# Twenty pairs of column blocks of h @ w_in, each by seven half products in place of eight, with gates and partial sums kept in DRAM and the convolution's norm moved behind the attention

## The chip, the cores and the metric

The kernel runs on one core of one Trainium2 chip. The metric is the device time of one launch in microseconds (us). Before the change two timed runs gave 2034.66 and 2035.71 us, so the median is 2035.18 us.

Engines are named as the profile names them: PE is TensorE (PEld its weight loads), DVE is VectorE, ACT is ScalarE, POOL is GpSimd, SP is SyncE, whose queue issues every DMA of this kernel.

## The reference, cut to what matters

Two layers (DEPTH 2) work on 512 tokens of 1024 channels in float32:

```python
h = rms_norm(x, norm_g)
z = h @ w_in                      # 1024 x 14848
(c_glu, c_gate, r_q, r_k, r_v, r_gate, a_q, a_k, a_v, a_gate, g_logit) = split(z)
y_conv = conv_module(c_glu, c_gate, ...) @ w_conv_out     # a*sigmoid(b), 31 taps, layer norm, silu, * silu(c_gate)
y_ret  = retention_branch(r_q, r_k, r_v, r_gate, ...) @ w_ret_out   # 4 heads, both directions, * silu(r_gate)
y_attn = window_attention_branch(...) @ w_attn_out        # 16 heads, 4 kv heads, window 128, * silu(a_gate)
g = sigmoid(g_logit + b_gate)
x = x + (g[0] * y_conv + g[1] * y_ret + g[2] * y_attn) @ w_out
```

## The kernel before, in words

**Products.** Every operand of a product is split into a high and a low part in the fp32r format (`hilo`, and for weights `weights`), and a product is the sum of three matmuls, high by high, high by low, low by high (`mm3`). A block of 128 output columns for all 512 tokens (`columns`, `proj`) takes 8 blocks of 128 input channels, so 24 matmuls with a 128x128 weight tile standing still and 512 tokens streaming through, all summed in one PSUM bank of the pool `pc`. Values, keys and queries are computed with the tokens on the partitions (`tokens`, `tokens256`); the queries' matmuls stream 256 columns, and there are 768 of them in the program.

**Weights.** The weights lie in DRAM in 156 blocks of 128x1024 a layer, in the order of use. One block is loaded by one DMA into `wraw` (3 buffers), its high part `wh` is made by ACT, its low part `wl` by DVE, each in one instruction of 128x1024.

**A layer.** `layer` runs four retention heads (`head`), then the convolution's norm (`conv_stats`, `conv_finish`), the attention (`attention`), and the merge and output projection (`finish`). `self.fill` names what is put between the stages of a head: the convolution's input blocks (`conv_in`: a pair of column blocks b and a, a tanh, a product, and 31 taps on DVE) and the gates of the convolution (`CG`). The retention's gate is four column blocks a head. `ATT_FILL` names what is put between the 16 steps of the attention: gates of the attention (A), merge gates (G), queries (Q) and the convolution's output projection (C). Results that are needed later, such as the taps' sums `y`, the gates and the partial sum `merged`, stay in SBUF.

**Order.** Nothing is issued in the order in which it is written. `Plan.record` notes each instruction with its place in the program (in ns of PE's work) and an offset of urgency; `Plan.order` then walks through a planned time, and lets each engine take the most urgent instruction whose operands are there and whose tiles have room, by the prices of `Plan.cost`. The result is one fixed order for each engine. Each engine then works through its own queue in order and waits on semaphores, so a late instruction holds up all behind it on its engine. Important offsets: loads are 20 us ahead of their place (LOAD_EARLY), weight splits 16 us, reads out of PSUM 20 us (EVAC_EARLY); the taps are 60 us late (TAPS_LATE), so they fill DVE's free time.

**Numbers in names.** `record` calls every instruction from one line, so all have line L318 in the profile (L334 after the change). They are told apart by their tiles: `pc` and `ps` are PSUM banks, `big` holds 128x4x512 arrays, `mid`, `pp` and `th` 128x512 tiles, `wide` the attention's scores, `pads` the padded rows for the taps.

Of the kernel before, what the change touches and what calls it, by code (L numbers as in the profile page):

```python
# [11 lines left out]
F32 = mybir.dt.float32  # L12
# [7 lines left out]
NK = D // P  # L20
EPS = 1e-6
# [13 lines left out]
LOAD_EARLY, SPLIT_EARLY, TAPS_LATE, STATS_LATE = -20000, -16000, 60000, 15000  # L35
# the order of the attention's gates (A), merge gates (G), queries (Q) and the convolution's projection (C) between its steps
ATT_FILL = ["C0", "C1 Q1", "C2", "C3", "C4", "C5 Q2", "C6", "C7", "A0 G0", "Q3 A1", "A2 G1", "A3 G2", "G3", "A4 G4", "A5 G5", "G6", "G7", "A6 A7"]

# columns of the combined input projection
# [4 lines left out]
# columns of the packed parameters  # L44
# [3 lines left out]
# columns of the packed constants  # L48
# [5 lines left out]
class View:  # L54
    """A part of a tile that is allocated when its first instruction is issued.

    ix holds the numbers of the elements that it covers, with the partitions in two halves."""
# [27 lines left out]
    def reshape(self, *shape):  # L85
        """Free dimensions split or joined in order."""
# [58 lines left out]
class Plan:  # L145
    """Records the instructions, orders them, and issues them to Tile in that order.

    Every engine takes, whenever it is free, the most urgent of the instructions whose operands are
    there and whose tiles have room; the engines take turns at a bank of PSUM. Urgency is the place in the program, in ns of the tensor
    engine's work, and an offset. Tiles with one tag are given room in the order of the program, so  # L150
    an order always exists."""


    def __init__(self, nc):
        self.nc = nc
        self.ops = []
        self.now = 0.0
        self.offset = 0.0
        for name in ("tensor", "vector", "scalar", "gpsimd", "sync"):
            setattr(self, name, Engine(self, name))  # L160
# [7 lines left out]
    def cost(self, engine, method, kw):  # L168
        out = kw.get("out")
        n = out.size if isinstance(out, View) else 0  # L170
        if method == "dma_start":
            return 60
        if engine == "tensor":
            if method == "transpose":
                return 107
            f32 = kw["rhs"].tile.dt == F32
            return max(n, 256 if n > 1 else 64) * (4 if f32 and n > 1 else 1) / 2.4
# [20 lines left out]
    def record(self, engine, method, kw):  # L198
# [8 lines left out]
        for writes, v in sorted(views, key=lambda x: x[0]):  # L207
# [3 lines left out]
            # a start of accumulation clears the whole bank's marks: it comes behind what the bank holds  # L211
# [29 lines left out]
    def order(self):  # L241
# [12 lines left out]
        while len(result) < len(ops):  # L254
# [4 lines left out]
            for e in names:  # L259
# [3 lines left out]
                if free[e] <= t:  # L263
# [15 lines left out]
                    if item is not None:  # L279
# [5 lines left out]
                        free[e] = t + op.cost  # L285
                        op.end = t + op.cost + (LATENCY if e != "sync" else 0)
# [3 lines left out]
                        if op.method == "dma_start":  # L290
                            n = max(v.size for v in op.args.values() if isinstance(v, View))
                            dma_free = max(dma_free, t) + n * P * 4 / 350
                            op.end = dma_free + 2000
# [39 lines left out]
class Pair:  # L333
    """A [128, 8, 512] array in two tiles of four rows each."""  # L334
# [4 lines left out]
    def __getitem__(self, k):  # L339
        return self.t[k // 4][:, k % 4, :]  # L340


class Builder:
    def __init__(self, nc, tc, ctx, io):
# [9 lines left out]
        self.pools["xd"] = Pool(ctx, tc, "xd", NK, space=bass.MemoryType.DRAM)  # L354

# [27 lines left out]
    def ps1(self):  # L383
        return self.tile("ps1", [P, S])

# [1 line left out]
    def weights(self, key):  # L387
# [3 lines left out]
        wh = self.tile("wh", [P, 1024], F32R)  # L391
        wl = self.tile("wl", [P, 1024], F32R)
        with nc.urgency(2 * FIRST + FIRST_STEP * (i - 0.1) if i < 4 else LOAD_EARLY):
            nc.sync.dma_start(out=raw, in_=self.io["wpk"][i])
        with nc.urgency(SPLIT_EARLY):
            nc.scalar.copy(out=wh, in_=raw)
            nc.vector.tensor_tensor(out=wl, in0=raw, in1=wh.bitcast(F32), op=ALU.subtract)
        return wh, wl

# [1 line left out]
    def mm(self, out, a, b, start, stop):  # L401
        self.nc.tensor.matmul(out=out, lhsT=a, rhs=b, start=start, stop=stop)

    def mm3(self, out, a, b, start, stop):
        """out (+)= (ah + al)^T (bh + bl), without al^T bl."""
        (ah, al), (bh, bl) = a, b
        self.mm(out, ah, bh, start, False)
        self.mm(out, ah, bl, False, False)
        self.mm(out, al, bh, False, stop)

    def columns(self, key, src, pool="pc"):
        """128 columns of src @ w, channels on partitions."""
# [10 lines left out]
    def rows(self, p, t, k, w, c):  # L423
        """adds the part of row k to 128 tokens' columns of src @ w_in."""
# [3 lines left out]
    def tokens(self, col):  # L428
        """512 columns of src @ w_in with tokens on partitions."""
# [8 lines left out]
    def tokens256(self, col):  # L438
        """256 columns of src @ w_in with tokens on partitions, two blocks of tokens in a bank."""
# [20 lines left out]
    def silu2(self, out, p):  # L460
        """2 silu(p) = (1 + tanh(p / 2)) p"""
        th = self.th()
        with self.nc.urgency(EVAC_EARLY):
            self.nc.scalar.activation(out=th, in_=p, func=AF.Tanh, scale=0.5)
            self.nc.vector.scalar_tensor_tensor(out=out, in0=th, scalar=1.0, in1=p, op0=ALU.add, op1=ALU.mult)

# [1 line left out]
    def rstd_of(self, acc, diag):  # L468
        """acc: [128, 512] sums of squares, to be added over the partitions."""
        nc = self.nc  # L470
        p = self.ps1()
# [8 lines left out]
        pr = self.ps1()  # L480
        self.mm(pr, self.ones, diag, True, True)
        return r, pr

# [27 lines left out]
    def new_input(self, l):  # L511
        """Room for a layer's input, scaled by the norm's gain and split."""
# [5 lines left out]
    def take(self, k):  # L518
        """x[k]: x[k] * g split, and its squares into the running sum."""
# [12 lines left out]
    def layer(self, l):  # L532
# [3 lines left out]
        self.merged = self.pair()  # L536
        CA = self.conv_in
        self.fill = {(0, 0): [lambda: CA(0)], (0, 1): [lambda: CA(1)], (0, 2): [lambda: CA(2)],
                     (1, 0): [lambda: CA(3)], (1, 1): [lambda: CA(4)], (1, 2): [lambda: CA(5)],
                     (2, 1): [lambda: CA(6)], (2, 2): [lambda: CA(7)],  # L540
                     (3, 1): [lambda: self.CG(0), lambda: self.CG(1)], (3, 2): [lambda: self.CG(2)]}
        for h in range(4):
            self.head(h, h == 0)
        self.conv_finish()
# [3 lines left out]
    def filler(self, *at):  # L548
        for f in self.fill.get(at, []):
            f()  # L550

    def normalise(self):
        """h = RMSNorm(x), split."""
        nc = self.nc
        self.rstd, pr = self.rstd_of(self.acc, self.pp())
# [6 lines left out]
        for k in range(NK):  # L562
            h = self.t2()
# [526 lines left out]
```

## Time and profile before

| what | value |
|---|---|
| timed runs | 2034.66 and 2035.71 us, median 2035.18 |
| span of the profiled execution | 2032.9 us, so 2.3 us of the median lie outside the span |
| PE busy, share of the span | 2021.1 us, 99% (9436 matmuls) |
| DVE busy | 1425.8 us, 70% |
| ACT busy | 834.9 us, 41% |
| DMA | 184.29 MB, mean 91 GB/s, 27.9% of the 16 engines' time for the main queue |
| granted TensorE clock | 1.000 |

The profile is of one execution. The page's first block gives busy times; the chain of work that ended last says which engine sets the end; the groups give, for each kind of instruction, its count, its total busy time and the mean time of one; the waits name who waited for whom; the timeline gives start times. Matmuls are pipelined: the profile gives a 128x512 matmul some 390 ns from start to end, though the next one starts about 230 ns later. The step from one start to the next is what a matmul costs, and it has to be taken from the timeline.

### The profile page before, as it was taken

What the parts mean: (1) busy time and instruction counts of PE and PEld (TensorE: products, weight loads), DVE (VectorE), ACT (ScalarE), POOL (GpSimd) and SP (SyncE); (2) the same over time, 40 slices, a digit from 0 to 9 for tenths busy, and PEclk for the clock granted to TensorE, in tenths of its full rate; (3) what the DMA queues carried; (4) which work ended last, traced back from release to release, by engine and by line L of the source; (5) the groups of instructions that cost most, each with busy time, mean ns of one, the idle gap of its engine ahead of it and who ended that gap; (6) DMA issues with size and microseconds to landing.
All of it is one profiled execution on the core that took longest, in us unless ns stands there. A gap on an engine that the chain in (4) does not pass through costs nothing.

```text
span 2032.9 us, 24260 instructions
## 1 busy us (share of the span) xinstructions
PE 2021.1 (99%) x9436; PEld 1661.8 (82%) x9436; DVE 1425.8 (70%) x2254; ACT 834.9 (41%) x1361; POOL 56.9 (3%) x62
## 2 busy tenths in 40 slices
PE   8999999999999999999999999999999999999999
PEld 6888888888788888888888888888888888888887
DVE  8788887588575556665567888875885755576652
ACT  5323223233344556673332332232333445566731
POOL 0000000000000000000000000000000000000000
PEclk9999999999999999999999999999999999999999
DMA  5322232222232222223432222222222322222232
GB/s 214 101 73 92 82 94 92 70 86 67 89 94 94 81 75 73 63 82 121 166 99 91 83 92 82 94 93 73 83 73 85 97 88 83 65 82 73 92 106 83
DMA packets 53683, 184.29 MB, mean 91 GB/s; under 512 B 6080, under 2 KB 6336, under 8 KB 53568
## 3 DMA queue, kind: packets, MB, share of 16 engines
q1 hardware_dynamic: 53568, 182.75, 27.9%
q8 instruction: 74, 1.21, 0.2%
q14 instruction: 41, 0.34, 0.0%
HBM read 178.53 MB, written 4.19 MB: 90 GB/s over the span
## 4 chain that ended last, share of the span: by engine, by line
PE 99%; DVE 0%; DMA 0%; issue 0%; ACT 0%; SPq 0%; DVEq 0%
PE pc L318 71%; PE ps L318 29%; DMA big<-xT 0%; DVE wl L318 0%; DVE wide L318 0%; SPq L318 0%; DVE pp L318 0%; ACT pp L318 0%; ACT big L318 0%; DVE sm_m L318 0%; DVEq L318 0%
## 5 line engine op out<-in xcount | busy, mean ns | idle before, releaser
L318 PE MATMUL pc<-big,wh 128*128 128x512 f32 x4096 | 1300.5, 397 | 0.0
L318 PEld LDWEIGHTS pc<-big,wh 128*128 128x128 f32 x4096 | 764.6, 188 | 177.8 <-issue 1.9
L318 PE MATMUL pc<-big,wl 128*128 128x512 f32 x2048 | 811.4, 396 | 0.3 <-DVE wl L318 0.3
L318 ACT CAST wh<-wraw 128x1024 fp32r<-128x1024 f32 x312 | 327.2, 1050 | 800.9 <-PE pc L318 531.9
L318 DVE TENSOR_TENSOR wl<-wraw,wh 128x1024 fp32r<-128x1024 f32 x312 | 380.6, 1222 | 212.0 <-ACT wh L318 210.3
L318 PEld LDWEIGHTS pc<-big,wl 128*128 128x128 f32 x2048 | 384.5, 188 | 91.1 <-DVE wl L318 0.8
L318 DVE SCALAR_TENSOR_TENSOR big<-pads,prm,big 128x512 f32<-128x512 f32 x480 | 340.4, 745 | 1.3
L318 PE MATMUL ps<-wh,big 128*128 128x512 f32 (+1 forms) x1152 | 295.4, 345 | 7.4 <-ACT big L318 7.4
L318 PEld LDWEIGHTS ps<-wh,big 128*128 128x128 f32 x1152 | 200.2, 189 | 35.6 <-ACT big L318 7.4
L318 PE MATMUL ps<-wl,big 128*128 128x512 f32 (+1 forms) x576 | 198.6, 346 | 0.0
L318 PEld LDWEIGHTS ps<-wl,big 128*128 128x128 f32 x576 | 108.9, 189 | 14.6 <-issue 0.5
L318 PE MATMUL ps<-big 128*128 128x512 f32 (+2 forms) x448 | 96.2, 344 | 0.2
L318 PEld LDWEIGHTS ps<-big 128*128 128x128 f32 x448 | 80.7, 188 | 15.6 <-DVE sm_m L318 0.9
L318 PE MATMUL ps<-big,pp 128*128 128x512 f32 x384 | 88.5, 389 | 0.0
L318 PEld LDWEIGHTS ps<-big,pp 128*128 128x128 f32 x384 | 72.1, 188 | 15.3
L318 DVE CUSTOM_DVE_ANT_0 wide<-ps,cst,prm 128x256 f32<-128x256 f32 (+1 forms) x128 | 66.1, 548 | 20.6 <-PE ps L318 19.9
L318 ACT CAST pp<-ps 128x512 fp32r<-128x512 f32 x80 | 46.0, 583 | 74.5 <-PE ps L318 73.9
L318 ACT ACTIVATE wide<-wide,sm_m 128x257 f32<-128x257 f32 (+1 forms) x128 | 70.5, 556 | 6.7 <-DVE sm_m L318 6.7
L318 DVE TENSOR_TENSOR big<-ps,big 64x512 fp32r<-64x512 f32 (+2 forms) x80 | 52.8, 662 | 26.0 <-ACT big L318 20.4
L318 DVE TENSOR_TENSOR pp<-ps,pp 128x512 fp32r<-128x512 f32 x80 | 54.3, 687 | 12.9 <-ACT pp L318 12.5
L318 ACT ACTIVATE wide<-wide,sm_d 128x256 f32<-128x256 f32 (+1 forms) x128 | 62.2, 557 | 2.0 <-DVE sm_d L318 2.0
L318 ACT ACTIVATE big<-mid 128x512 fp32r<-128x512 f32 x64 | 40.0, 630 | 39.0 <-DVE mid L318 39.0
(98 smaller groups left out, 1255.5 us busy)
## 6 DMA issues: line engine op xcount, KB each, us to landing
wraw<-wpk SPq DMA_DIRECT2D x312, 512.0 KB, 3.5
wide<-toe SPq DMA_DIRECT2D x16, 448.0 KB, 3.4
big<-xT SPq DMA_DIRECT2D x8, 256.0 KB, 5.1
pp<-xT SPq DMA_DIRECT2D x8, 256.0 KB, 4.3
xd<-big SPq DMA_DIRECT2D x8, 256.0 KB, 2.0
pp<-xd SPq DMA_DIRECT2D x8, 256.0 KB, 4.5
out<-pp SPq DMA_DIRECT2D x8, 256.0 KB, 2.0
cst<-cst SPq DMA_DIRECT2D x1, 832.0 KB, 7.9
```

The lines of the kernel that those rows point to most:

```text
L318: getattr(getattr(self.nc, op.engine), op.method)(**kw)
```

## The change

In `two`, a pair of column blocks (two times 128 columns, 1024 input channels, 512 tokens) is treated as a 2x2 by 2x2 product: the channels in two halves, the two column blocks, the tokens in two halves of 256. Strassen's scheme needs seven half products where eight are plain. A half product is 4 blocks of channels by three matmuls of 256 tokens: 12 matmuls, so 84 matmuls of 256 in place of 48 of 512. In return sums are needed: `two` makes four sums of weight halves (`ws`, DVE), splits seven halves of 512 (ACT and DVE), and combines the products in five reads of PSUM by DVE and two by ACT, 256 wide; `sums` makes the sums of the token halves once a layer, in place of h in `x`, and splits them (`th_`, `tl_`). 20 pairs a layer go this way: the convolution's inputs (8), the retention's gates (8), the convolution's gates (4). They are named C, R and S in `HEAD_FILL`, and all lie beside heads 0 and 1.

Along with it:

- `keep` writes a 128x512 tile to DRAM, `fetch` reads it back. So go the conv's inputs (`vd`), the retention's gates (`rg`), the convolution's gates (`cg`), merge gates (`g0`, `g2`), the taps' sums (`y`, `yc`), two heads' outputs (`og`), and the partial sums (`m1`, `m2`, `md`, `oa`): 432 DMAs of 256 KB more in all, on SP's queue.
- All weights are split in halves of 512; `wraw` has 4 buffers, `wh` and `wl` 8 of half the size; `big` has 12 tiles where it had 15, `mid` 2 where it had 3; the single bank `ps1` joins `pc`, which then has 4.
- silu is one activation (Silu) for the gates and the convolution's output, with 11 further ACT_TABLE_LOADs; before it was a tanh on ACT and a product on DVE.
- The convolution's norm is done in four steps (`conv_stats`, X0 to X3) between steps of the attention, and its output projection comes last, in `finish`, behind the attention's. The merge gates of the convolution (L) move into the heads.
- The planner prices DMAs, table loads and matmuls a little differently (matmuls at 2.2 columns a ns where it was 2.4); TAPS_LATE is 150 us.

```diff
-POOLS = {"big": 15, "pp": 8, "mid": 3, "th": 2, "wide": 2, "pads": 1, "wraw": 3, "wh": 3, "wl": 3}
-PSUM_POOLS = {"pc": 3, "ps": 4, "ps1": 1}
+POOLS = {"big": 12, "pp": 8, "mid": 2, "th": 2, "wide": 2, "pad": 1, "yt": 2, "wraw": 4, "wh": 8, "wl": 8, "ws": 2, "half": 3}
+PSUM_POOLS = {"pc": 4, "ps": 4}
...
+HEAD_FILL = {(0, 0): "L0 L1 L2", (0, 1): "R0 R1 C0 C1 T0", (0, 2): "C2 C3 C4 C5 R2 R3",
+             (1, 0): "T1", (1, 1): "C6", (1, 2): "C7 S0", (1, "o"): "R4 R5 R6 R7 S1 S2 S3", (2, 0): "T2", (2, 1): "T3", (2, 2): "T4",
+             (3, 0): "T5", (3, 1): "T6 T7 L3 L4", (3, 2): "L5 L7"}
...
+    def two(self, col0, col1, out0, out1, func=None):
+        r0, r1 = (self.raw(("ct", self.l, c)) for c in (col0, col1))
...
+        def product(p, w, x, row, side, first=False):
+            for j in range(4):
+                c = slice(j * P, (j + 1) * P)
+                self.mm3(p[:, left], (w[0][:, c], w[1][:, c]), tuple(v[row + j][:, side] for v in x), first and j == 0, j == 3, not first)
+        a11 = self.split(r0[:, lo])
+        s1 = add(sa[:, lo], r1[:, lo], r1[:, hi])
+        s2 = add(sa[:, hi], sa[:, lo], r0[:, lo])
+        s3 = add(sb[:, lo], r0[:, lo], r1[:, lo])
+        a12 = self.split(r0[:, hi])
+        s4 = add(sb[:, hi], sa[:, hi], r0[:, hi])
+        a22 = self.split(r1[:, hi])
+        a, b, e = self.pc(), self.pc(), self.ps()
+        product(a, a11, hs, 0, left, True)
+            nc.scalar.copy(out=t1, in_=a[:, left])
+        product(b, s2, ts, 4, right, True)
+            nc.vector.tensor_tensor(out=v2, in0=b[:, left], in1=t1, op=ALU.add)
+        product(e, s1, ts, 0, left, True)
+            nc.vector.tensor_tensor(out=t51, in0=e[:, left], in1=t1, op=ALU.add)
+        product(a, a12, hs, 4, left)
+                nc.scalar.activation(out=out0[:, left], in_=a[:, left], **func)
+        product(b, s3, ts, 0, right)
+            nc.vector.scalar_tensor_tensor(out=out1[:, right], in0=b[:, left], scalar=-1.0, in1=t51, op0=ALU.mult, op1=ALU.subtract)
+        product(e, s4, hs, 4, right)
+            nc.vector.tensor_tensor(out=out0[:, right], in0=e[:, left], in1=v2, op=ALU.add)
+        product(b, a22, ts, 4, left)
+            nc.vector.scalar_tensor_tensor(out=out1[:, left], in0=b[:, left], scalar=-1.0, in1=t1, op0=ALU.mult, op1=ALU.subtract)
...
+    def keep(self, name, i, src):
+        self.kept[name, i] = self.tile(name, [P, S])
+        self.nc.sync.dma_start(out=self.kept[name, i], in_=src)
...
+    def fetch(self, name, i, dst=None, again=False):
+        with self.nc.urgency(LOAD_EARLY):
+            dst = self.pp() if dst is None else dst
+            self.nc.sync.dma_start(out=dst, in_=self.kept[name, i] if again else self.kept.pop((name, i)))
```

**Three places of the order.** The first is PE's queue at the tightest point of a pair, before its last half product; the pair is one of the retention's gates (R) beside head 1's output projection. Bank `pc_3802` holds b: its product with s3 ends, then come 12 matmuls of s4 in bank `ps_3823` (the last four are shown), one matmul of another column block (`pc_3902`), and then the product with a22 in `pc_3802` again, which may start only when DVE has read the bank.

```order
L334 MATMUL ps_3823<-big_512,wl_3750 128x256
L334 MATMUL ps_3823<-big_512,wh_3738 128x256
L334 MATMUL ps_3823<-big_523,wh_3738 128x256
L334 MATMUL ps_3823<-big_512,wl_3750 128x256
L334 MATMUL pc_3902<-big_3431,wh_3784 128x512
L334 MATMUL pc_3802<-big_863,wh_3760 128x256
L334 MATMUL pc_3802<-big_888,wh_3760 128x256
```

Before the change no PSUM bank was written again after a read within a product: a gate's block held one bank for its 24 matmuls and was read when they were done.

The second place is DVE's queue in that same pair. `ws` are the sums of weights, `wl` the low parts, `half` and `pp` the reads of PSUM, `yt` the taps.

```order
L334 TENSOR_TENSOR wl_3858<-wraw_3644,wh_3827 128x512
L334 TENSOR_TENSOR wl_3865<-ws_3779,wh_3846 128x512
L334 SCALAR_TENSOR_TENSOR yt_2812<-pad_2768,prm_205,yt_2812 128x512
L334 TENSOR_TENSOR wl_3884<-ws_3779,wh_3868 128x512
L334 SCALAR_TENSOR_TENSOR pp_3893<-pc_3802,half_3853 128x256
L334 TENSOR_TENSOR wl_3898<-ws_3789,wh_3887 128x512
L334 TENSOR_TENSOR pp_3874<-ps_3823,half_3830 128x256
L334 SCALAR_TENSOR_TENSOR yt_2812<-pad_2768,prm_205,yt_2812 128x512
```

Before, this is what stood in DVE's queue beside the gates of head 1 (`big_1653` is the gate, `big_685` the taps' sum):

```order
L318 SCALAR_TENSOR_TENSOR big_1653<-th_1680,pc_1622 128x512
L318 SCALAR_TENSOR_TENSOR big_685<-pads_153,prm_176,big_685 128x512
L318 TENSOR_TENSOR wl_1695<-wraw_1524,wh_1671 128x1024
L318 SCALAR_TENSOR_TENSOR big_685<-pads_153,prm_176,big_685 128x512 x3
L318 TENSOR_TENSOR wl_1723<-wraw_1570,wh_1710 128x1024
L318 SCALAR_TENSOR_TENSOR big_1653<-th_1719,pc_1669 128x512
```

So where the taps filled most of DVE's queue, low parts and reads of PSUM now stand, with a tap here and there. The read `pp_3893<-pc_3802`, for which PE waits at the first place, has the low part `wl_3884` right ahead of it.

The third place is SP's queue beside the same pair, where only weight loads stood before:

```order
L334 DMA wraw_3848<-wpk 128x1024
L334 DMA rg_3924<-pp_3874 128x512
L334 DMA wraw_3932<-wpk 128x1024
L334 DMA rg_3943<-pp_3893 128x512
L334 DMA wraw_3965<-wpk 128x1024
L334 DMA m1_3994<-pp_3981 128x512
```

Each write to DRAM waits in this queue until its tile is finished, and the weight load behind it waits with it.

More of the change, by code (lines that the diff above doesn't have):

```diff
@@ L158, in __init__ @@
         self.offset = 0.0
+        self.table = None
         for name in ("tensor", "vector", "scalar", "gpsimd", "sync"):
@@ L284, in order @@
                         op.start = t
-                        free[e] = t + op.cost
-                        op.end = t + op.cost + (LATENCY if e != "sync" else 0)
+                        func = op.args.get("func")
+                        load = 0
+                        if func in (AF.Exp, AF.Silu) and func != self.table:
+                            self.table, load = func, 1300
+                        free[e] = t + op.cost + load
+                        op.end = free[e] + (LATENCY if e != "sync" else 0)
                         for x in op.tiles:
@@ L458, in hilo, with silus, rstd_diag @@
             nc.vector.scalar_tensor_tensor(out=lo, in0=src, scalar=scale, in1=hi.bitcast(F32), op0=ALU.mult, op1=ALU.subtract)
[L460 to L468, printed above, removed]
+    def silus(self, name, k, col):
+        out = self.pp(), self.pp()
+        self.two(col, col + P, *out, dict(func=AF.Silu))
+        self.nc.scalar.activation(out=out[1], in_=out[1], func=AF.Silu)
+        for i in range(2):
+            self.keep(name, k + i, out[i])
+    def rstd_diag(self, acc, diag):
         nc = self.nc
-        p = self.ps1()
+        p = self.pc()
         for t in range(4):
@@ L669, in head @@
             self.hilo(Ph[j], Pl[j], pf)
-        gate = self.t8()
-        for kt in range(4):
-            self.silu2(gate[:, kt, :], self.proj(R_GATE + h * 512 + kt * P))
+        if first:
+            self.sums()
         pv = [self.ps() for t in range(4)]
@@ L693, in head, with put, other @@
         self.filler(h, 1)
+        src = [None] * 8, [None] * 8
+        def put(c, og, tiles):
+            for part, t in zip(src, tiles):
+                part[c] = t[:, c % 4, :]
+            self.hilo(src[0][c], src[1][c], og)
+        def other():
+            parts = self.t8(F32R), self.t8(F32R)
+            for kt in range(4):
+                put(kt, self.fetch("og", kt), parts)
         if h == 3:
-            self.conv_stats()
-        ogh = self.t8(F32R)
-        ogl = self.t8(F32R)
+            other()
+        if h % 2:
+            parts = self.t8(F32R), self.t8(F32R)
         for kt in range(4):
@@ L778, in conv_finish @@
[L778 to L797 removed]
+        hi, lo = self.pair(F32R), self.pair(F32R)
@@ L880, in attention @@
         nc, prm = self.nc, self.prm
+        self.kv()
+        for m in range(4):
+            self.G1(m)
+        self.Q(0)
+        for m in range(4, 8):
+            self.G1(m)
         V, kTh, kTl = self.V, self.kTh, self.kTl
-        self.g2 = self.pair()
         self.og = self.pair()
@@ L967, in finish, with part @@
         og = self.og
-        ogh = self.pair(F32R)
-        ogl = self.pair(F32R)
+        ogs = self.pair(F32R), self.pair(F32R)
         for k in range(8):
-            self.hilo(ogh[k], ogl[k], og[k], 0.5)
+            self.hilo(ogs[0][k], ogs[1][k], og[k], 0.5)
+        def part(kind, gate, src, m):
+            p = self.columns((kind, l, m), src)
+            t = self.fetch(gate, m)
+            with nc.urgency(EVAC_EARLY):
+                nc.vector.scalar_tensor_tensor(out=t, in0=t, scalar=1.0, in1=p, op0=ALU.add, op1=ALU.mult)
+            return t
+        for m in range(8):
+            t = part("oa", "g2", ogs, m)
+            md = self.fetch("md", m)
+            nc.vector.tensor_tensor(out=t, in0=t, in1=md, op=ALU.add)
+            self.keep("oa", m, t)
+            if m == CONV_AT:
+                yg = self.conv_finish()
         mh = self.pair(F32R)
```

310 lines of the change are left out of this document (180 added, 130 removed).

## The prediction, made before the changed kernel ran

> **What bounds the kernel now.** I read the page first: busy times, then the chain that ended last.
>
> ```profile
> span 2032.9 us, 24260 instructions
> ...
> PE 2021.1 (99%) x9436; PEld 1661.8 (82%) x9436; DVE 1425.8 (70%) x2254; ACT 834.9 (41%) x1361; POOL 56.9 (3%) x62
> ...
> PE 99%; DVE 0%; DMA 0%; issue 0%; ACT 0%; SPq 0%; DVEq 0%
> ```
>
> PE is the chain. A busy share of 99% alone could hide waits, since a matmul's end is modelled, so I asked the waits next, of PE and of SP's queue.
>
> ```profile
> PE ps L318 <- ACT big L318: 7.4, 1, 7.4
> PE pc L318 <- DVE wl L318: 0.3, 2, 0.2
> ```
> ```profile
> SPq L318 <- DVE wl L318: 1691.3, 298, 17.5
> ```
>
> PE waits 7.4 us at the start, for the first operand, and 0.3 us in all the rest. SP's loads wait until DVE's split frees a buffer (`wl`): the weights are ahead of PE. So the time is the sum of the steps from one matmul's start to the next one's. The timeline gives these steps; a fence holds the first and the last row of a stretch, in which a row of two `wh` and a row of one `wl` take turns.
>
> ```profile
> 960.13 0.63 PE L318 MATMUL pc<-big,wh 128*128 128x512 f32 x2
> ...
> 965.73 0.63 PE L318 MATMUL pc<-big,wh 128*128 128x512 f32 x2
> ```
>
> Between these starts lie 24 matmuls of 512: 5.60 / 24 = 233.3 ns each. The queries' matmuls are the only long streams of 256, two stretches of them:
>
> ```profile
> 628.09 0.40 PE L318 MATMUL ps<-wh,big 128*128 128x256 f32 x2
> ...
> 631.27 0.40 PE L318 MATMUL ps<-wh,big 128*128 128x256 f32 x2
> ```
> ```profile
> 1826.61 0.39 PE L318 MATMUL ps<-wh,big 128*128 128x256 f32 x2
> ...
> 1829.33 0.39 PE L318 MATMUL ps<-wh,big 128*128 128x256 f32 x2
> ```
>
> 27 in 3.18 us are 117.8 ns each; in the later stretch 24 in 2.72 us are 113.3 ns. Half the width costs half, so seven half products are worth having.
>
> **PE's gain.** A pair of blocks is 48 x 233.3 = 11.20 us before and 84 x 117.8 = 9.90 us after: 1.30 us less, and 40 pairs make 52.1 us. With the later stretch's 113.3 it would be 67.2. No other matmul is added or dropped. I take 117.8, the slower row. The break-even step is 11.20 / 84 = 133.3 ns.
>
> The Trainium skill speaks against this change: "TensorE: Matmul & The Clock Gate", section "Back-to-back issue gap", gives for a stream of weight load and matmul about 81 ns at 128 columns and 131 at 512, since both operations set the step. A straight line between its figures gives 98 at 256 (an estimate), so 8.2 us for 84 against 6.3 for 48: the change would lose 77 us. This trace has 233.3 and 117.8, where half is half, so the measurement speaks for the change; the rule's way out is a rival below.
>
> **DVE pays.** Its instructions overlap a little, so I use starts again:
>
> ```profile
> 256.61 4.72 DVE L318 SCALAR_TENSOR_TENSOR big<-pads,prm,big 128x512 f32<-128x512 f32 x7
> 261.25 1.22 DVE L318 TENSOR_TENSOR wl<-wraw,wh 128x1024 fp32r<-128x1024 f32 x1
> 262.38 3.40 DVE L318 SCALAR_TENSOR_TENSOR big<-pads,prm,big 128x512 f32<-128x512 f32 x5
> ...
> 964.55 0.69 DVE L318 TENSOR_TENSOR mid<-mid,big 128x512 f32<-128x512 f32 x1
> 965.16 1.22 DVE L318 TENSOR_TENSOR wl<-wraw,wh 128x1024 fp32r<-128x1024 f32 x1
> ```
>
> A tap takes 4.64 / 7 = 0.66 us, a low part of 1024 1.13, a two-tensor instruction of 512 0.61. A read of PSUM that is 256 wide has its nearest row here:
>
> ```profile
> L318 DVE TENSOR_TENSOR big<-ps,mid 64x256 f32<-64x256 f32 x64 | 26.6, 416 | 1.6 <-ACT mid L318 0.8
> ```
>
> A pair has 7 low parts and 4 sums of 512 (11 x 0.61) and 5 such reads (5 x 0.42): 8.8 us of DVE beside 9.9 of PE. Before, it had two low parts of 1024 and one or two reads at 0.61 to 0.69: 3.2 us. That is 5.6 x 40 = 224 us more. The other 232 weight blocks in halves cost 2 x 0.61 - 1.13 = 0.09 each, 21 us; the sums of the token halves and their low parts 4 x 1.13 + 8 x 0.61 a layer, 19 us; the convolution's inputs keep their product, no longer out of PSUM, 16 x 0.61 = 10 us; one multiplication less in the convolution's norm saves 16 x 0.66 = 11. DVE goes from 1426 to about 1,690 us, 85% of the new time. All pairs stand beside heads 0 and 1, some 300 us of PE a layer; counting DVE's instructions that the order puts there, at these steps, I get some 270 us, 90%. That this much can be hidden shows here:
>
> ```profile
> 150.00:200.00 50.00, 50.00 (x219) 40.63 (x218) 44.55 (x63) 16.11 (x21) 0.00 (x0) 1.00 0.30 94
> ```
>
> In 50 us DVE (44.55) is 89% busy, and PE has none free: 219 matmuls in 50 us are the 228 ns a step of its mix. The cover of DVE's work is thus PE's stream, and if DVE needed over 100% of a stretch, all above would be on the path.
>
> **The wait inside a pair.** PE must wait until DVE has read b after s3. Between stand 12 or more matmuls of 256, at least 12 x 117.8 = 1.41 us. The matmul ends 0.28 us after its start, 0.16 after the next one's, then comes at most one DVE instruction that is under way (0.61) and the read (0.42): 1.19 us. It is hidden, with 0.2 us to spare. If DVE comes two instructions late, PE loses 0.4 to 0.5 us, in 40 pairs 20 us. Behind a waiting matmul stands all of PE.
>
> **The attention gets shorter, not its side work.** Of the column blocks between its 16 steps 15 move away (the convolution's output projection and seven of its merge gates), 15 x 24 x 0.2333 = 84 us of PE a layer.
>
> ```profile
> 655.00:740.00 85.00, 85.00 (x459) 72.54 (x458) 49.83 (x104) 49.88 (x103) 4.31 (x5) 1.00 0.25 81
> 740.00:815.00 75.00, 74.89 (x410) 63.93 (x408) 47.20 (x97) 43.44 (x88) 4.31 (x5) 1.00 0.22 71
> 815.00:895.00 80.00, 79.84 (x439) 68.52 (x439) 51.34 (x114) 54.78 (x117) 4.23 (x9) 1.00 0.23 73
> ```
> ```profile
> L318 ACT CAST wh<-wraw 128x1024 fp32r<-128x1024 f32 x312 | 327.2, 1050 | 800.9 <-PE pc L318 531.9 <-issue 152.6 <-PE ps L318 83.5
> ...
> L318 ACT ACTIVATE th<-pc,prm 128x512 f32<-128x512 f32 x32 | 22.0, 687 | 2.5 <-PE pc L318 2.3
> ```
>
> Over these 240 us DVE and ACT (148 us each) were 62% busy. With the blocks go 15 low parts and 15 instructions of 512 from DVE (15 x 1.13 + 15 x 0.65 = 27 us), 15 high parts and 7 tanh from ACT (15 x 1.05 + 7 x 0.69 = 21 us); the norm's steps come in (22 of 0.61, 13 us of DVE, and 8 squares, each at most a tanh, 6 us of ACT): about 134 us each for 156 us of PE, 86%. PE has fewer matmuls to put between a step's scores and its softmax. What that costs shows at one place of before, where little stood between:
>
> ```profile
> 812.17 1.95 PE L318 MATMUL ps<-big 128*128 128x384 f32 x8
> 813.96 0.63 PE L318 MATMUL pc<-big,wh 128*128 128x512 f32 x2
> 814.42 0.60 PE L318 MATMUL ps<-cst,wide 128*128 128x128 f32 x4
> 815.18 0.50 PE L318 MATMUL pc<-big,wl 128*128 128x512 f32 x1 [0.16 <-DVE wl L318]
> ```
>
> 8 matmuls of 384 at three quarters of 233.3 ns, 2 of 512 and 4 of 128 (at most 0.44 us together) are 2.3 us; they took 3.0. So 0.7 us were lost, once a layer. After the change I take four such places a layer, 8 x 0.7 = 5.6 us. The bounds: none, and all 32 steps, 22 us.
>
> **DRAM and the rest.** 432 more DMAs of 256 KB are 113 MB, so 297 MB, near 149 GB/s. The start of the kernel moved far more:
>
> ```profile
> 15.00:20.00 5.00, 5.00 (x23) 4.11 (x22) 5.00 (x10) 3.30 (x7) 0.00 (x0) 1.00 1.03 408
> ```
> ```profile
> wraw<-wpk SPq DMA_DIRECT2D x312, 512.0 KB, 3.5
> ...
> pp<-xd SPq DMA_DIRECT2D x8, 256.0 KB, 4.5
> ```
>
> A read of 256 KB lands in 4.5 us, a weight block in 3.5; both are asked for 20 us ahead, which hides them as it hides the weights now. If a write that waits in SP's queue used up that lead, PE would stand still. The 11 table loads fall to an ACT that has room. I put 2 us on the pairs and these together.
>
> **The sum.** 2032.9 - 52.1 + 5.6 + 2 = 1988.4 us of span; the median of the timed runs lies 2.3 above the span, so 1990.7: I predict 1991 us, 2.2% less. A measurement of this kernel can tell about 2% from no change; that line is at 1994.5, so close that the lost places decide.
>
> **Rivals.**
>
> 1. DVE and ACT keep losing PE time (20 us in the pairs, two instructions late each, and half of the attention's bound, 11): 2035.2 - 52.1 + 31 = 2014 us, no clear change. For it: 90% and 86% are more than any long stretch of before, and reads that must wait for PE leave holes in DVE's queue. Against it: PE lost nothing at 89%.
> 2. Weight loads come late. Place: SP's queue, where each pair's two loads stand behind writes that wait for ACT or DVE. Price: one landing, 3.5 us, not hidden in each of 40 pairs: 2035.2 - 52.1 + 140 + 8 = 2131 us, slower. It decides once a pair loses over 1.30 us there. For it: before, no write stood among the loads of this stretch. Against it: SP waited 1691 us for buffers, so loads have lead, and now there are 4 buffers.
> 3. The step of 256 is set by the weight load, which lasts 188 ns:
>
> ```profile
> L318 PEld LDWEIGHTS ps<-wh,big 128*128 128x128 f32 x1152 | 200.2, 189 | 35.6 <-ACT big L318 7.4 <-issue 0.5
> ```
>
> Were these not overlapped in a pair, 84 x 0.189 = 15.9 us against 11.20 a pair: 2035.2 + 187 + 8 = 2230 us; from 133.3 ns a step on the change loses. The queries' loads overlap, so it is unlikely. This is where the skill's rule named above would lead.
> 4. Strassen's scheme is not done as often as it says: the order has 3360 more matmuls of 256 and 1920 fewer of 512, so I give it nothing.
>
> **How the numbers follow.** My forecast has 0.57, rival 1 0.37, rival 2 0.04, rival 3 0.02. Faster by over 2%: 0.57. Within 2%: 0.37. Slower by over 2%: 0.06. The range begins at the 113.3 ns step with nothing lost, 2035.2 - 67.2 = 1968, rounded to 1970, and ends where rival 1 has the whole of its bounds: 2035.2 - 52.1 + 20 + 22 = 2025.
>
> **What would show it.** Right: 256-wide rows of `pc` at about 118 ns a step, PE busy near 1,975 us, DVE near 1,690, DMA near 297 MB, PE's waits under 10 us beside the start, most of them in the attention. Wrong: steps of 256 over 125 ns in the pairs; PE's waits for DVE reads of `pc` over 15 us (rival 1); waits for `wraw` (rival 2).

## The result, and the profile after

The changed kernel takes 1968.05 us (two timed runs, 1967.55 and 1968.56), 67.1 us less than before: ratio 0.967, 95% interval 0.9642 to 0.9698. That is faster by over 2%, as forecast (2.2%), but 23 us under the forecast's 1991 and just outside its range. The profile page of the changed kernel:

```profile
span 1965.8 us, 29855 instructions
...
PE 1954.4 (99%) x10876; PEld 1693.2 (86%) x10876; DVE 1670.2 (85%) x3004; ACT 1000.8 (51%) x1900; POOL 60.7 (3%) x90
...
DMA packets 115922, 297.91 MB, mean 152 GB/s; under 512 B 12992, under 2 KB 13248, under 8 KB 115776
...
PE 99%; DMA 1%; DVE 0%; ACT 0%; issue 0%; SPq 0%; DVEq 0%; ACTq 0%
```

DVE (1670, 1690 forecast) and DMA (298 MB, 297 forecast) are near what was worked out; PE's busy time is 21 us under the 1975. All of PE's waits:

```profile
PE ps L334 <- ACT big L334: 7.1, 1, 7.1
PE ps L334 <- DVE sm_m L334: 0.2, 1, 0.2
```

So the time is still the sum of PE's steps, and the missing 23 us must be steps. The timeline, first and last row of four stretches; in the first, 36 matmuls of 256 lie between the starts, in the second 60, in the third and fourth 24 of 512:

```profile
274.54 0.40 PE L334 MATMUL ps<-big,wh 128*128 128x256 f32 x2
...
278.78 0.40 PE L334 MATMUL ps<-big,wh 128*128 128x256 f32 x2
...
312.41 0.39 PE L334 MATMUL pc<-big,wh 128*128 128x256 f32 x2
...
319.21 0.39 PE L334 MATMUL ps<-big,wh 128*128 128x256 f32 x2
...
562.11 0.62 PE L334 MATMUL pc<-big,wh 128*128 128x512 f32 x2
...
567.60 0.62 PE L334 MATMUL pc<-big,wh 128*128 128x512 f32 x2
...
885.08 0.63 PE L334 MATMUL pc<-big,wh 128*128 128x512 f32 x2
...
890.68 0.63 PE L334 MATMUL pc<-big,wh 128*128 128x512 f32 x2
```

4.24 / 36 = 117.8 ns and 6.80 / 60 = 113.3: the pairs have both steps that the queries had before. But the plain blocks, 5.60 / 24 = 233.3 before, now have 5.49 / 24 = 228.8 in the heads and 5.60 / 24 = 233.3 in the finish. The forecast had left them as they were. All steps of the two traces, from one start to the next, summed by width:

| width | before: matmuls, sum of steps us | after | difference |
|---|---|---|---|
| 512 | 7851, 1838.1 | 5931, 1381.0 | -457.1 |
| 256 | 896, 105.3 | 4256, 498.6 | +393.3 |
| 128 and 384 | 656, 74.7 | 656, 71.7 | -3.0 |

The counts are those of rival 4: 1920 matmuls of 512 fewer, 3360 of 256 more.

Steps that are longer than the normal one of their width by over 40 ns lose 15.2 us in all before and 16.5 after: the lost places of the attention (5.6) and the 2 us in the pairs did not come. The stretches that were to show them, in the pairs (100 to 150) and in the attention (columns: PE, PEld, DVE, ACT, POOL busy, granted clock, DMA):

```profile
700.00:750.00 50.00, 50.00 (x306) 44.11 (x305) 39.60 (x98) 38.36 (x89) 4.10 (x5) 1.00 0.25 80
...
800.00:850.00 50.00, 50.00 (x258) 41.81 (x257) 42.70 (x104) 45.35 (x108) 1.89 (x5) 1.00 0.34 114
100.00:150.00 50.00, 49.88 (x425) 49.68 (x424) 46.67 (x87) 27.09 (x52) 0.00 (x0) 1.00 0.57 189
```

DVE is 93% busy in the pairs, DVE and ACT up to 85 and 91% in the attention, and PE misses at most 0.12 us in 50.

### The profile page after: what moved, and what is told of

The parts are those of the page before. It is cut to its first block, busy times and chain, and to the rows that moved or that the text cites. A ratio compares the mean times of both kernels' runs of the same rounds, so it can differ in the third digit from the quotient of the medians.

```text
span 1965.8 us, 29855 instructions
## 1 busy us (share of the span) xinstructions
PE 1954.4 (99%) x10876; PEld 1693.2 (86%) x10876; DVE 1670.2 (85%) x3004; ACT 1000.8 (51%) x1900; POOL 60.7 (3%) x90
## 4 chain that ended last, share of the span: by engine, by line
PE 99%; DMA 1%; DVE 0%; ACT 0%; issue 0%; SPq 0%; DVEq 0%; ACTq 0%
PE pc L334 64%; PE ps L334 35%; DMA wraw<-wpk 0%; DMA big<-xT 0%; DMA yt<-y 0%; DVE wl L334 0%; DVE pp L334 0%; ACT wh L334 0%; SPq L334 0%; DVE ws L334 0%; DVE qk_v L334 0%; ACT pp L334 0%; ACT big L334 0%; DVE wide L334 0%; DVE yt L334 0%
## 5 line engine op out<-in xcount | busy, mean ns | idle before, releaser
L334 PE MATMUL pc<-big,wh 128*128 128x512 f32 (+1 forms) x4416 | 1181.0, 353 | 0.1
L334 PE MATMUL pc<-big,wl 128*128 128x512 f32 (+1 forms) x2208 | 779.3, 354 | 0.0
L334 ACT CAST wh<-wraw 128x512 fp32r<-128x512 f32 x584 | 361.0, 621 | 633.9 <-PE pc L334 436.8
L334 DVE TENSOR_TENSOR wl<-wraw,wh 128x512 fp32r<-128x512 f32 x584 | 397.2, 687 | 79.6 <-ACT wh L334 76.7
L334 DVE SCALAR_TENSOR_TENSOR yt<-pad,prm,yt 128x512 f32<-128x512 f32 x480 | 358.5, 747 | 5.5
L334 ACT CAST wh<-ws 128x512 fp32r<-128x512 f32 x160 | 99.3, 622 | 114.0 <-PE pc L334 68.3
L334 PEld LDWEIGHTS ps<-wl,big 128*128 128x128 f32 x576 | 108.9, 189 | 15.2 <-issue 0.2
L334 PE MATMUL ps<-big,wh 128*128 128x256 f32 x640 | 115.7, 279 | 0.0
L334 DVE TENSOR_TENSOR wl<-ws,wh 128x512 fp32r<-128x512 f32 x160 | 108.3, 685 | 4.0 <-ACT wh L334 2.7
L334 PEld LDWEIGHTS ps<-big,wh 128*128 128x128 f32 x640 | 97.4, 188 | 0.1
L334 PE MATMUL ps<-big,wl 128*128 128x256 f32 x320 | 89.1, 279 | 0.0
```

What stands on the lines that cost most here:

```text
L334: getattr(getattr(self.nc, op.engine), op.method)(**kw)
```

## The experiments

The theory: the sum of PE's steps is the time; the pairs' gain is as forecast, and something in the rest of the change shortened other steps. Rivals: the pairs gave all of it; DVE or the queue still cost time that hides a larger gain. All times are medians, beside a kernel before of 2034.5 to 2035.0 each time.

| run | us | ratio to before, 95% |
|---|---|---|
| plain_pairs | 2013.8 | 0.9883 to 0.991 |
| no_weight_sums | 1970.3 | 0.967 to 0.9696 |
| sums_half | 1981.5 | 0.9721 to 0.9747 |
| sums_twice | 2044.2 | 1.0033 to 1.0058 |
| pairs22 | 1976.3 | 0.9703 to 0.9729 |
| att_less8 | 2003.8 | 0.9832 to 0.9859 |
| keep_twice | 1962.3 | 0.9633 to 0.9659 |
| halves_before | 2038.9 | 1.0009 to 1.0028 |
| before_layout | 2010.8 | 0.987 to 0.9897 |
| mm_order | 1963.9 | 0.9639 to 0.9666 |
| before_aligned | 1994.8 | 0.9792 to 0.9818 |
| plain_aligned | 1992.8 | 0.9781 to 0.9808 |
| after_aligned | 1961.1 | 0.9627 to 0.9653 |
| plain_192 | 2032.5 | 0.9982 to 1.0 |
| after_192 | 1976.0 | 0.9698 to 0.9725 |
| after_offsets | 1952.4 | 0.9585 to 0.9611 |

### The pairs alone, the rest alone

```diff
 def two(self, col0, col1, out0, out1, func=None):
+    p0 = self.columns(("ct", self.l, col0), (self.hh, self.hl))
+    p1 = self.columns(("ct", self.l, col1), (self.hh, self.hl))
+    nc.scalar.activation(out=out0, in_=p0, **func)
+    nc.scalar.copy(out=out1, in_=p1)
```

> The changed kernel with all 40 pairs computed plainly (two blocks of 24 matmuls of 512, two reads of PSUM by ACT), without the sums of the token halves and of the weights; DRAM, pools, order and the late norm stay. Theory: PE's steps are all there is, the scheme gives 40 x (48 x 232.8 - 84 x 117.05 ns) = 54 us, and the other 13 us of the gain came with the rest of the change: about 2022 us (2014 if the plain blocks step at 229 ns). Rival A, the rest of the change gives nothing and the scheme all 67 us: 2035. Rival B, the forecast's own terms, the rest costs 7.6 us that the scheme pays for: 2042.

2013.8, the expectation's sum for blocks at 229 ns: the scheme is worth 45.7 us here, and the rest of the change, which the forecast had costing 7.6, brings 21 of its own. In its trace the blocks step at 229 ns in the heads, as in the changed kernel. So the question became what shortens a step.

### DVE and the queue

no_weight_sums leaves out the sums (`return self.split(b)`), so its products are of other weights; sums_twice writes each sum twice, sums_half two of the four:

```diff
 def add(out, a, b):
-    nc.vector.tensor_tensor(out=out, in0=a, in1=b, op=ALU.add)
+    for i in range(2):
+        nc.vector.tensor_tensor(out=out, in0=a, in1=b, op=ALU.add)
```

> The changed kernel without the four sums of weight halves in a pair (the halves themselves are split in their place, so the products are of other weights): 160 DVE instructions of 0.61 us, 98 us, less. Theory: DVE is not on the path, its work is covered by PE's stream: 1968 us within 3. Rival, DVE at 92 to 96% in the pairs holds PE up: the time falls by up to 20 us, to 1948.

> The changed kernel with two of the four sums of weight halves in a pair written twice: 80 DVE instructions more, 49 us. Theory, DVE stands at its ceiling already, as the 98 us that cost 76 and the two pairs more a layer say: some three quarters of it are lost, 37 us, about 2005. Rival, there is slack of some 20 to 25 us, which the 98 us used up first: 49 - 22 = 27 us, 1995; with the slack all at places that this load doesn't need, 1968 to 1980.

> The changed kernel with each of the four sums of weight halves in a pair written twice: 160 DVE instructions more, 98 us, DVE 90% of the span. Theory: the taps that fill DVE's free time beside the pairs move to where there is room, PE loses under 20 us: 1968 to 1988. Rival, a pair's own DVE work is the limit: at 8.8 + 2.4 = 11.2 us against 9.8 of PE it loses 1.4 us a pair, 56 us, 2024; if DVE was at its limit already, all 98 us, 2066.

At 0.61 us a sum, 98 us less of DVE gain nothing (1970.3), 49 more cost 13.4, 98 more cost 76.1 (in the traces DVE's busy time changes by 90, 43 and 92 us). So the change ends just short of a bend, by the first of these losses some 36 us of DVE away (49 - 13). The theories of sums_twice (under 20 us lost) and of sums_half (37) were both wrong: sums_twice lies between its rival's two sums, 2024 and 2066, and sums_half just above its rival's lower range, 1968 to 1980. That the taps could not move to where DVE has room, as the theory of sums_twice had it, may be the reason; no run tested it. The first waits of PE in sums_twice (7.4 us of the second is the start), and the stretch from 100 to 150 us, where PE was busy for 49.88 us in the changed kernel:

```profile
PE pc L334 <- DVE wl L334: 13.1, 10, 1.9
PE ps L334 <- ACT big L334: 12.5, 2, 7.4
PE ps L334 <- DVE pp L334: 9.9, 8, 2.9
```
```profile
100.00:150.00 50.00, 44.48 (x352) 43.81 (x352) 43.71 (x80) 27.69 (x49) 1.39 (x1) 0.93 0.42 135
```

Not all of the 76 us are waits. PE's waits beside the start sum to some 45 us, and the granted clock, 1.00 in the changed kernel, was 0.987 in the mean of this run: an estimate of 26 us more, 1.3% of its 2043.

pairs22 takes two more pairs a layer:

```diff
-... "R4 R5 R6 R7 S1 S2 S3"), ... (3, 1): "T6 T7 L3 L4", (3, 2): "L5 L7"
+... (1, 2): "C7 S0 P0", (1, "o"): "R4 R5 R6 R7 S1 S2 S3 P1", ... (3, 1): "T6 T7", (3, 2): ""
```

> The changed kernel with two more pairs a layer: the merge gates L3 and L4, L5 and L7 by the scheme, beside head 1, where they stood plain beside head 3. PE's steps: 4 x (11.17 - 9.83) = 5.4 us less. Theory, DVE stands at its ceiling from head 0 to the attention (98 us more of it cost 76 us): 4 x 5.6 = 22 us more of DVE cost some 17, the sum is 12 us slower, about 1980. Rival, each pair saves 1.3 us as the 20 do: about 1963.

1976.3 is near the first number, but for another cause. PE's long steps sum to 31.9 us in place of 16.5, and the increase stands at two places, 541 and 1522 us, once a layer:

```profile
541.14 0.48 PE L334 MATMUL ps<-cst,big 128*128 128x128 f32 x1 [4.89 <-ACT big L334]
```

These are head 3's transposes, which wait for the normalised heads: the gates that left head 3 had covered that. Behind the wait the granted clock was 0.5 until 545.6 us, which adds to the 4.89 us. In the pairs nothing was lost, so DVE's ceiling is not what this run showed; without the 15 us it would stand at 1961, beside the rival's 1963.

keep_twice doubles each write:

```diff
     self.nc.sync.dma_start(out=self.kept[name, i], in_=src)
+    self.nc.sync.dma_start(out=self.tile(name + "_2", [P, S]), in_=src)
```

> The changed kernel with every tile that goes to DRAM written twice (a second copy that nobody reads): 57 MB more, on the same queue. Theory: the queue and DRAM have room, 1968 us within 3. Rival, weight loads come late behind the writes: over 1975.

1962.3 with 352 MB in place of 298: not slower, so the traffic costs nothing that shows. That it is 5.8 us faster is taken up below.

### The attention's cover

```diff
-ATT_FILL = ["L6", "Q1", "G0", "G1", "G2 X0", "A0 Q2", "A1", "G3 X1", "G4", "Q3", "A2", "A3", "G5", "A4", "G6 X2", "A5", "G7 X3", "A6 A7"]
+ATT_FILL = ["L6", "Q1", "", "", "X0", "A0 Q2", "A1", "X1", "", "Q3", "A2", "A3", "", "A4", "X2", "A5", "X3", "A6 A7"]
+(2, 0): "T2 G4 G5", (2, 1): "T3 G6 G7", (2, 2): "T4 G0 G1", (3, 0): "T5 G2 G3"
```

> The changed kernel with the eight merge gates of the attention's branch (G0 to G7) moved from between the attention's steps to heads 2 and 3: 8 x 24 matmuls, 45 us of PE a layer, no longer stand there. Theory: PE loses nothing between the steps while DVE and ACT need less time than PE, and the rest when they need more: 111 us of PE against some 124 of DVE a layer, 13 us lost, 26 in both: about 1994. Rival A, the forecast's price, a loss that grows with each block taken out (7.6 us for 30 blocks): about 1972. Rival B, the blocks hide nothing there: 1968 within 3.

2003.8, 36 us slower: the cover does matter. The 30 blocks that the change took out cost about 1 us, these 16 more cost 36, so a price for each block taken away was the wrong form. The trace points to the work at one place, and not to that of the whole attention: from 695 to 895 us DVE was 81% and ACT 78% busy, but where PE stood still, one of them was full (DVE 9.78 of 10 us from 740, 9.89 from 825; ACT 9.67 from 835). PE's waits beside the start sum to 24 us, near the 26 expected. The rest is the granted clock: it was 0.5 in five stretches of 3.4 us, which is an estimate of 8.5 us lost. Two of the five lie in this stretch, at 833 and 840 us, and make its mean 0.93 (1.00 in the changed kernel):

```profile
800.00:850.00 50.00, 47.33 (x281) 40.86 (x280) 41.77 (x108) 40.05 (x96) 6.10 (x9) 0.93 0.19 59
```

### What sets a step

Three single edits: the weights of the kernel before split in halves (`wh` and `wl` 6 tiles of 512 each); its pools in the opposite order; in the changed kernel, the order of the second and third matmul of a product.

```diff
-POOLS = {"big": 15, "pp": 8, "mid": 3, "th": 2, "wide": 2, "pads": 1, "wraw": 3, "wh": 3, "wl": 3}
+POOLS = {"wl": 3, "wh": 3, "wraw": 3, "pads": 1, "wide": 2, "th": 2, "mid": 3, "pp": 8, "big": 15}
```
```diff
-self.mm(out, ah, bl, False, False, more)
-self.mm(out, al, bh, False, stop, more)
+self.mm(out, al, bh, False, False, more)
+self.mm(out, ah, bl, False, stop, more)
```

> The kernel before with one edit: each weight block split in two halves of 512 (6 buffers each for high and low parts) in place of one of 1024. Theory 1, the halves are not what made the remaining blocks' step fall from 233.3 to 229.0 ns: 2035 us within 3, the step of 512 stays at 233 to 234 ns. Theory 2, the halves are it: the step falls to 229 in the heads and the time by 7 to 30 us, 2005 to 2028.

> The kernel before with one edit: its SBUF pools laid out in the opposite order, so that every tile has another address; each engine's instructions stand in the same order. Theory 1, a matmul's step follows the addresses of its operands: the step of the column blocks leaves 233.3 ns (226 to 236 were seen), the time moves by 7 to 40 us. Theory 2, addresses don't matter: 2035 us within 3, and 233.3 ns.

> The changed kernel with the second and third matmul of each three changed over: high by high, low by high, high by low, so two neighbours share the second operand in place of the first. Theory 1, the step depends on the sequence of loads and not on the shape alone: the steps of 512 and 256 move by several ns, the time by more than 5 us, to either side. Theory 2, the shape sets it: 1968 us within 3.

The halves do nothing for the step (2038.9, with one wait of 3.1 us for DVE; the blocks stay at 233.3). The turned layout, with every engine's instructions in the same order, takes 24 us off the kernel before. Its timeline in the finish, 24 matmuls between the starts:

```profile
941.55 0.39 PE L318 MATMUL pc<-big,wl 128*128 128x512 f32 x1
...
947.27 0.62 PE L318 MATMUL pc<-big,wh 128*128 128x512 f32 x2
...
952.76 0.62 PE L318 MATMUL pc<-big,wh 128*128 128x512 f32 x2
```

5.49 / 24 = 228.8, where the kernel before had 233.3. So addresses count. mm_order gave 4.2 us, between its two theories; it is taken up below. The next two runs measure addresses alone:

```diff
+for k in range(8):
+    for j, (w, v) in enumerate(((wh, xh), (wh, xl), (wl, xh))):
+        nc.tensor.matmul(out=p[:, 0:width], lhsT=big[:, w + 128 * k:w + 128 * k + 128], rhs=big[:, v + 512 * k:v + 512 * k + width], ...)
```

> No part of the layers: one SBUF tile of 204 KB a partition, and streams of 48 matmuls of 512 (weight load and matmul as in a column block) whose four operands (high and low weights, high and low channels) lie at chosen addresses, 45 choices, once in one order and once in the reverse, with no other engine at work; then four streams of 256. The output is one bank of products. Theory 1, addresses set the step: the streams with the addresses of the kernel before step at 233 ns, those of the turned layout and of the changed kernel's heads at 229, the same in both orders, and the moves of one operand tell which distance matters. Theory 2, addresses act only through what other engines do at the time: all streams have one step.

> No part of the layers: the streams of the run on addresses again, 48 matmuls each, now at widths 512, 256 and 128, with the distance of moving operand to weights going from 0 to 224 modulo 256 bytes in steps of 32, for two absolute places of the moving operand, in both orders. Theory: the step is a function of width and distance alone, with the best distance for 512 at 0 (226.7 ns; 128 gives 232, 192 gives 233.3) and for 256 at 192 (113.3; 0 gives 120.0, 64 gives 117.8), the same at both places. Rival: the absolute places count too, and the two places differ.

Shifting the weights or the channels by 256 bytes or one of the multiples tried (up to 32768) changes nothing, by 64 or 128 it does, and both places of the moving operand (the channels, in a column block) give one curve, up to the entries with two steps below: what counts is the distance, the moving operand's address less the stationary one's, modulo 256 bytes. One row of the timeline for each stream of distances, second order (512 wide at distance 0, 64, 128, 192; 256 wide at 0, 64, 192), then 256 at 192 in the first order, and 128 wide at 0. A row's length less the last matmul's (0.39 or 0.28), divided by its count less one, is the step:

```profile
505.83 8.55 PE L58 MATMUL pc<-big 128*128 128x512 f32 x37
483.65 8.63 PE L58 MATMUL pc<-big 128*128 128x512 f32 x37
460.83 8.52 PE L58 MATMUL pc<-big 128*128 128x512 f32 x36
438.62 8.56 PE L58 MATMUL pc<-big 128*128 128x512 f32 x36
421.79 4.48 PE L58 MATMUL pc<-big 128*128 128x256 f32 x36
410.82 4.40 PE L58 MATMUL pc<-big 128*128 128x256 f32 x36
387.72 4.52 PE L58 MATMUL pc<-big 128*128 128x256 f32 x37
151.80 4.47 PE L58 MATMUL pc<-big 128*128 128x256 f32 x38
376.83 4.41 PE L58 MATMUL pc<-big 128*128 128x128 f32 x38
```

| distance | 512 wide, ns | 256 wide, ns |
|---|---|---|
| 0 | 226.7 | 120.0 |
| 64 | 228.9, in one stream 233.3 | 117.8 or 113.3 |
| 128 | 232 to 233 | 118.8 |
| 192 | 233.3 | 117.8 or 113.3 |

Multiples of 32 between these give 233 to 234 and 116.7 to 120; 128 wide steps at 111.6 at every distance. Three entries hold two steps, and a stream keeps one of them from its first half to its second. At distance 64, 55 of the 56 streams of 512 in the two runs stepped at 228.9 and one at 233.3. That one stood behind a stream of 233.3, but so did six that stepped at 228.9; so the stream before does not decide it. What picks the step stays open, and with it why the heads and the finish of the changed kernel differ at one distance, and what inside the chip does this.

In the kernel before, `wide` (tiles of 4 x 385 numbers, 6160 bytes) ahead of the weights puts them 192 from the channels. In the changed kernel `pad` (542 numbers, 2168 bytes) adds to it, and the distance is 64. That is most of the 21 us: the steps of the 7851 matmuls of 512 sum to 1838 us before and to 1821 in plain_pairs, where those of the column blocks that lost nothing have a mean of 230.1 ns in place of 233.3. Another 3 us are in the steps of 128 and 384.

### The test in the whole kernel

The layout alone is set, with the same order of instructions on every engine as in the run it is compared with:

```diff
-before  "th": 2, "wide": 2, "pads": 1, "wraw": 3, "wh": 3, "wl": 3
+before_aligned (0)  "th": 2, "wraw": 3, "wh": 3, "wl": 3, "wide": 2, "pads": 1
-after, plain_pairs  "th": 2, "wide": 2, "pad": 1, "yt": 2, "wraw": 4, "wh": 8, "wl": 8, "ws": 2, "half": 3
+after_aligned, plain_aligned (0)  "th": 2, "yt": 2, "wraw": 4, "wh": 8, "wl": 8, "ws": 2, "half": 3, "wide": 2, "pad": 1
+after_192, plain_192 (192)  "th": 2, "wide": 2, "yt": 2, "wraw": 4, "wh": 8, "wl": 8, "ws": 2, "half": 3, "pad": 1
```

> The kernel before with two pools moved to the end of the list, wide and pads, whose tiles are no multiple of 256 bytes long: the weights then lie at 128 modulo 256 bytes as the channels do (192 before); every engine's instructions stand in the same order. Theory, the step is set by the distance of a matmul's two operands modulo 256 bytes (0: 226.7, +64: 228.9, -64: 233.3 ns in the streams): the steps of 512 go to 226.7 ns, 7851 of them 45 us less, 896 of 256 some 4 less, about 1986. Rival, only the exact places count: 2035 within 3, or something between that fits no distance.

> The changed kernel with the pools wide and pad moved to the end of the list, so that weights (64 modulo 256 bytes before) and channels both lie at 128; the same order on every engine. Theory: 512 at 226.7 (5931 steps, 25 us less), 256 at 113.3 (4256 steps, 14 us less): 1929 if DVE keeps up; a PE faster by 2% asks of DVE what 34 us more work did, which costs some 8 us by the doubled sums: 1929 to 1940. The aligned kernels then differ by 40 x (48 x 226.7 - 84 x 113.3 ns) = 54 us less that loss. Rival, DVE's ceiling takes most of the gain: 1950 to 1968.

> The changed kernel with the 40 pairs computed plainly, as before, and with weights and channels aligned (distance 0). Theory: it differs from the aligned changed kernel by 40 x (48 x 226.7 - 84 x 120.0 ns) = 32 us, 1993, near the aligned kernel before, 1994.8: once the addresses are the same, the rest of the change is worth nothing. Rival, the late norm and the rest bring something of their own: below 1988; they cost something: over 2000.

> The changed kernel with plain pairs and only its pool pad moved to the end of the list, which puts weights and channels at the distance that they had in the kernel before (192). Theory: the other parts of the change are worth nothing at equal addresses, so it takes what the kernel before takes, 2035 within 4. Rival, they cost the forecast's 7.6 us: 2042; they bring the 21 us: 2014.

> The changed kernel with the same move of the pool pad, so with the distance of the kernel before (192). Theory: 512 steps at 233.3 ns and 256 at 113.3 or 117.8, both of which this distance has: the pairs give 40 x (48 x 233.3 - 84 x 117.8) = 52 us to 67, and the time is 1968 to 1983. Rival, the forecast's lost places come on top where the step isn't shorter: 1976 to 1991.

Steps in the finish of before_aligned (24 matmuls between the starts) and in the pairs of after_aligned (69):

```profile
930.30 0.62 PE L318 MATMUL pc<-big,wh 128*128 128x512 f32 x2
...
935.74 0.62 PE L318 MATMUL pc<-big,wh 128*128 128x512 f32 x2
```
```profile
129.97 0.40 PE L334 MATMUL pc<-big,wh 128*128 128x256 f32 x2
...
138.25 0.40 PE L334 MATMUL pc<-big,wh 128*128 128x256 f32 x2
```

512 came down to 226.7 as expected, but 256 went up to 120.0, which no expectation had before these two runs. At 6.7 ns a matmul that is 6 of the 9 us by which before_aligned missed its 1986, and 28 of the 32 by which after_aligned missed its 1929. With the curve known, plain_aligned (1993 expected) and both runs at 192 came where they should. In plain_192 the column blocks are back at a mean of 233.3 ns. The 1976.0 of after_192 lies in the range of its rival too, but its long steps sum to no more than the changed kernel's, so the rival's lost places are not there. The same change at three distances:

| distance | plain pairs | with the scheme | scheme worth |
|---|---|---|---|
| 192, as before | 2032.5 | 1976.0 | 56.5 |
| 64, as changed | 2013.8 | 1968.05 | 45.7 |
| 0 | 1992.8 | 1961.1 | 31.7 |

At equal addresses the rest of the change is worth next to nothing: 2032.5 against 2034.7, 1992.8 against 1994.8, some 2 us, about what the steps of 128 and 384 lost.

Last, each width at its own distance, the plain blocks at 0 and the pairs and queries at 192:

```diff
+wh = self.tile("wh", [P, 576], F32R)[:, at:at + 512]   # at = 0; 16 in the pairs, 48 for the queries
```

> The aligned changed kernel with one more shift: the weights of the pairs start 64 bytes and those of the queries 192 bytes into their tiles, so that the distance of moving operand to stationary one is 0 for widths of 512 and 384 and 192 for 256; tiles are 256 bytes longer, and 7 buffers of each kind take the place of 8. Theory: 512 stays at 226.7, 256 falls from 120.0 to 113.3 where the fast one of its two steps at this distance holds: 1961 - 4128 x 6.7 ns = 1933; with the slow one, 117.8, 1952. Rival: DVE, 92 to 96% busy in the pairs, can't follow, or 7 buffers are too few: over 1961.

1952.4, the fastest of all, with 512 at 226.7 and most of 256 at the slower of its two steps, 117.8 (mean of all 256, 117.3).

## Why the prediction was right and wrong

- **PE's gain, 52.1 us.** Right in kind and nearly in size: 56.5 at the addresses from which its rows came; the matmuls of the pairs have a mean step of 115.9 there, where I took the slower row's 117.8 (6 us). Where the changed kernel really stands, the blocks that the pairs replace step at 230.1 in the mean (plain_pairs), and the gain is 45.7.
- **"No other matmul is added or dropped."** This is the step that failed. It was true, and I took it to mean that all other matmuls keep their time. The pool list, which I read as room only, moved the weights from distance 192 to 64. In the kernel with plain pairs that is about 19 us (2032.5 to 2013.8), in the changed one 7.9 (1976.0 to 1968.05): it has fewer matmuls of 512, and its column blocks fell less, from 233.3 to 230.7 in the mean. Without these 7.9 us the time, 1976.0, would lie inside my range.
- **The lost places, 5.6 us, and 2 us for the pairs and DRAM.** The second step that failed: 7.6 us forecast, 1.3 more us of long steps measured. The mechanism exists, but in att_less8 it shows at places where DVE or ACT was 97 to 99% busy over 10 us; 86% of a stretch is not that, and I charged a price for it all the same.
- **The sum.** From 1990.7 to 1976.0, at the addresses of before: 7.6 that the losses did not take, 4.4 from the pairs, 2.7 by which plain_192 is below the 2035.2. From there to 1968.05, the addresses. That 1968 is also what I got for 113.3 ns in every pair and nothing lost, before I rounded that end of the range to 1970, is a coincidence: that sum has 67.2 us from the pairs, and the pairs gave 45.7.
- **Rival 1** (DVE and ACT lose 31 us): no, but it was closer than DVE's 85% of the span sounds: 49 us more work cost 13.
- **Rival 2** (late loads): no wait of PE for `wraw`, and 55 MB more cost nothing (keep_twice).
- **Rival 3** (the weight load sets the step of 256): no, 113.3 to 120.0 in every run. The estimate of 98 ns from the Trainium skill, "TensorE: Matmul & The Clock Gate", section "Back-to-back issue gap", does not hold here. Of its two figures, 81 ns at 128 columns and 131 at 512, neither does: the streams show 111.6 and 226.7 to 234.
- **A few us that no term explains.** keep_twice and mm_order are 4 to 6 us faster than the changed kernel, and no_weight_sums 2 slower, with the same matmuls on PE. At distance 64 the mean step of the column blocks is 230.7 in the changed kernel and 229.4 in the first two, since more of them caught 228.9; in no_weight_sums more matmuls of 256 caught 117.8. At that distance such differences say nothing of the edit.

## What to carry to other kernels

Before a change that alters pools or tile sizes is priced from steps in the old trace, compare the addresses of matmul operands modulo 256 bytes on both sides; a reordered pool list alone gave 40 us here (before_aligned). A loss from missing cover is a bend, not a price per block: look for places of some 10 us in which another engine would be full, since the mean of a long stretch hides them (81% in att_less8), and ask which stretch a moved block had been covering. To find what an idea is worth, undo only the idea and leave its surroundings.

## What the runs showed of the hardware

- A 128x512 fp32r matmul with a weight load steps at 226.7 to 234 ns and a 128x256 one at 113.3 to 120.0, by the distance of its operands modulo 256 bytes, where 512's best distance, 0, is 256's worst; at some distances one of two steps holds for a whole stream, and what picks it stays open.
- The granted clock was 0.5 for 3.4 us at a time behind lost time on PE: twice in 50 us of att_less8 in which PE lost at most 1.3 us at once (so 0.93 in the mean), and for 6.8 us in and after the 4.89 us wait of pairs22. So a wait costs more than its length. The Trainium skill, "TensorE: Matmul & The Clock Gate", section "What's actually happening", speaks of an idle window of about 3.4 us; in att_less8 there was none, only shorter, scattered waits: some 2 to 2.7 us lost in the 3.4 us before each of the two.
